# First FFN's end in a two-layer transformer on one NeuronCore: normalised tiles scaled by VectorE and transposed plainly, instead of multiplied by a scaled identity

## The chip, the cores and the metric

The kernel runs on one core of one Trainium2 chip. The metric is device time in microseconds (us) for one execution; less is better. The engines of the core have short names in the profile: PE is TensorE (matmuls; PEld is its weight load), DVE is VectorE, ACT is ScalarE, POOL is GpSimd and SP is SyncE, which here only issues DMAs. Each engine works through its own queue in order, and waits on semaphores where a result of another engine is needed.

## The reference

Two layers over 768 tokens (256 context, 512 latent) of width 1024. Each layer has a mixer and a SwiGLU feed-forward block (FFN), each between two RMS norms:

```python
def _rms(x, gain, eps=1e-6):
    y = xf * lax.rsqrt(jnp.mean(xf * xf, axis=-1, keepdims=True) + eps)
    return y * gain
def _modulate(h, shift, scale):
    return h * (1 + scale) + shift
...
x_lat = x_lat + m_lat[5] * _rms(_swiglu(h_lat, w_gate, w_up, w_down), norm_post_ffn[l])
...
h_lat = _modulate(_rms(x_lat, norm_pre_mix[l]), m_lat[0], m_lat[1])   # next layer
o_ctx, o_lat = _odd_mixer(h_ctx, h_lat, ...)                          # starts with h @ w_in
```

The change is at the seam of the two layers: the end of the first FFN (last assignment), and the norm, modulation and transposition that make `h`, the input of the second layer's mixer.

## The kernel before, in words

Tokens are worked in six tiles of 128, in the order 4, 5 (context), 0, 1, 2, 3 (latent). Products are made in a split form: every float32 operand is a high part and the rest ("H" and "L", `fp32r`), and each product is three matmuls (`mm3`: H by H, H by L, L by H).

The **down product** of the first FFN (`down`) is seven passes of a Strassen scheme. Its result gathers in one tile `y`, [128, 6, 1024], a row of 1024 per token tile, in SBUF. The sixth pass finishes `y` for tiles 4, 5 and 0; the seventh and last finishes it for 1, 2 and 3 (L1798, `y<-y,x`). For each finished tile, `end` queues a small chain of work, `post_pre`:

- a DMA on SP loads the residual, `xr<-x` (L1512; four buffers for six tiles),
- `post_norm`: ACT sums the squares of `y` (L676), DVE multiplies by the gate row (`pn<-y,gv`, L746), DVE scales the sum (`ms`, L666), POOL takes the power -1/2 (`rs`, L668), DVE makes `xr = pn*rs + xr` (L755); for latent tiles SP stores it (L1515),
- `pre_norm`: ACT sums the squares of `xr` (L676), DVE and POOL make a second `rs`, and then DVE multiplies the 128x128 identity by `rs`, a row each: `dg` (L689). When two tiles of a pair (4 and 5, 0 and 1, 2 and 3) are ready, their transposition is queued.

`pair_turn` transposes a pair in four steps `q`. In a step PE makes four 128x128 products of a block of `xr` (the stationary operand) and `dg` (the moving one) into one PSUM tile `hT`: that is the transposed block, each token scaled by its `rs`. ACT applies the modulation (two L727, `hf<-hT`) and casts the high part (L734), DVE makes the low part (L735). Only then can the next layer read these 256 columns of the two tiles. `hT` has two PSUM buffers.

The steps are strewn among other matmuls of PE, and this order is written out by hand. The four steps of the pair 4, 5 stand among the last matmuls of the down product's seventh pass (`x`). Then comes `values`, the first product of the second layer's mixer (`nat`): for each of two column halves `c` and each token tile, 24 matmuls over four weight units `i` (each a DMA `raw<-in_odd_w_in`, an ACT cast `wH` L769 and a DVE subtraction `wL` L770). The steps of pair 0, 1 stand in the second token tile of `c = 0`, one after each weight unit; the steps of pair 2, 3 in the fourth. Behind them, DVE sums a modulation vector (`macc`, L595 and L597) from weights that SP loads (L579), and PE turns it near the end of `values` (`mod_acc`).

PE's order and that of DVE, ACT and POOL in this part are those of the program text (they are pinned there); DMAs of SP are placed by the tile framework, by when their buffer comes free.

The normalisation ahead of the FFNs (`forms` in the code) already works with a whole scaled tile: DVE writes `xn = xr * rs` (L695), and PE transposes blocks of it with the plain identity (L358).

Of the kernel before, what the change touches and what calls it, by code (L numbers as in the profile page):

```python
# [8 lines left out]
F32 = mybir.dt.float32  # L9
# [4 lines left out]
ALU = mybir.AluOpType  # L14
# [3 lines left out]
P = 128  # L18
D = 1024
# [297 lines left out]
class Net:  # L317
# [358 lines left out]
        self.nc.scalar.activation(junk, src, AF.Square, accum_out=ss)  # L676
        return ss

    def pre_norm(self, pool, t, xt, A, B, h):

        nc = self.nc
        r = 0 if t < LT else 1
        forms = isinstance(h, Forms)
        xn = pool.tile([P, D], F32, tag="xn", bufs=2, name=f"xn{t}") if forms else None
        rs = self.rstd(self.sumsq(xt, xn), D)
        yield
        if not forms:
            dg = pool.tile([P, P], F32, tag="dg", bufs=4, name=f"dg{t}")
            self.mark = nc.vector.tensor_scalar(dg, self.ident, rs, None, op0=ALU.mult)  # L689
            self.pair.append((xt, dg))  # L690
            if len(self.pair) == 2:
                self.turns.append(self.pair_turn(pool, t - 1, self.pair, A, B, h))
                self.pair = []
            return
        self.mark = nc.vector.tensor_scalar(xn, xt, rs, None, op0=ALU.mult)  # L695

        def turn():
            for hf in range(2):
                pt = self.tr_tile(f"hT{t}{hf}")
                f = h.at(hf, t)  # L700
                for kk in range(4):
                    k = hf * 4 + kk
                    self.tr(pt[:, kk * P : (kk + 1) * P], xn[:, k * P : (k + 1) * P], self.ident)
                for kk in range(4):
                    k = hf * 4 + kk
                    src = pt[:, kk * P : (kk + 1) * P]
                    nc.scalar.activation(f[:, kk, :], src, AF.Identity, bias=B[:, r, k : k + 1], scale=A[:, r, k : k + 1])
                h.put(hf, t)

        self.turns.append(turn)  # L710

    def pair_turn(self, pool, t, pair, A, B, h):

        nc = self.nc
        r = 0 if t < LT else 1
        tok = slice(t * P, t * P + 2 * P)

        for q in range(4):
            pt = self.tr_tile(f"hT{t}{q}").rearrange("p (k i) -> p k i", k=2)
            f = pool.tile([P, 2, 2 * P], F32, tag="hf", bufs=2, name=f"hf{t}{q}")  # L720
            for kk in range(2):
                k = 2 * q + kk
                for a, (xt, dg) in enumerate(pair):
                    self.mm(pt[:, kk, a * P : (a + 1) * P], xt[:, k * P : (k + 1) * P], dg, start=True, stop=True)
            for kk in range(2):
                k = 2 * q + kk
                nc.scalar.activation(f[:, kk, :], pt[:, kk, :], AF.Identity, bias=B[:, r, k : k + 1], scale=A[:, r, k : k + 1])  # L727
            self.latest = self.put(h, slice(2 * q, 2 * q + 2), tok, f)
            if q < 3:
                yield  # L730
# [777 lines left out]
    def post_pre(self, pp, y, t, gvs, xsrc, xdst, nxt, cuts):  # L1508

        nc = self.nc  # L1510
        xt = pp.tile([P, D], F32, tag="xt", bufs=4 if nxt and isinstance(nxt[2], Split) else 2, name=f"xr{t}")
        nc.sync.dma_start(out=xt, in_=xsrc(t))  # L1512

        def store(c):
            nc.sync.dma_start(out=xdst(t)[:, c], in_=xt[:, c])  # L1515

        yield from self.post_norm(y, xt, gvs[0 if t < LT else 1], cuts, xdst and store)
        if nxt is not None:
            A, B, h = nxt
            yield from self.pre_norm(pp, t, xt, A, B, h)  # L1520

    def turn(self, left=0):

# [676 lines left out]
```

## Time and profile before

| | us |
|---|---|
| median of 3 runs | 1691.47 (1688.34 to 1691.84) |
| the profiled execution | 1689.01 |
| its span, first to last instruction | 1686.9 |
| granted TensorE clock, mean | 0.998 |
| PE busy | 1646.0 |
| DVE busy | 1309.3 |
| ACT busy | 920.0 |
| down product's last pass, to values' start | 885.7 to 914.1 |
| first and last matmul with `dg` | 905.2 and 945.0 |
| end of the last `dg` | 933.3 |

A row of a timeline has the start in the span, the length, the engine, the line, the operation, output and inputs by the program's names, the shape, how many equal ones it merges, and in brackets for how long the engine stood idle before it and what ended that. A matmul's length is longer than the distance to the next one, because they are pipelined: starts are what to compare. A `q` behind an engine's name is its queue issuing something.

### The profile page before, as it was taken

Reading aid. Unit: us, or ns where it says so; the run is one execution under the profiler, and the core shown is the slowest. Engines: PE = TensorE matmul, PEld = TensorE weight load, DVE = VectorE, ACT = ScalarE, POOL = GpSimd, SP = SyncE. Lnnn points to the kernel's source line nnn. Section 1 sums busy time; section 2 is a strip of 40 time slices with the busy share of each in tenths; the row PEclk is TensorE's granted clock in tenths of the full one; section 3 lists DMA queues with packets and bytes.
Section 4 is the critical chain, followed back from the end, with each engine's and each line's share of the span. In section 5 each row is a group of like instructions: output and inputs, shape, how many; then the busy total and the mean of one; then the engine's idle time right before and its main releaser. Section 6 shows DMA issues by size and latency. Waiting matters only on the chain.

```text
span 1686.9 us, 32540 instructions
## 1 busy us (share of the span) xinstructions
PE 1646.0 (98%) x13407; PEld 1481.6 (88%) x13407; DVE 1309.3 (78%) x2105; ACT 920.0 (55%) x1560; POOL 124.4 (7%) x129
## 2 busy tenths in 40 slices
PE   7999998999999999999999999999999999999997
PEld 5889987888999999998887888888888899999875
DVE  4889768875898988878667548788774599987987
ACT  4745567836543443445447436566664565555654
POOL 1004210011000000003102000000000100000221
PEclk9999999999999999999999999999999999999999
DMA  9651002164243444348625542121124333333793
GB/s 329 192 155 41 2 27 101 51 211 152 85 140 102 148 149 140 113 149 175 131 91 197 177 125 61 51 64 39 52 65 149 125 113 114 112 101 101 190 198 137
DMA packets 184736, 204.79 MB, mean 121 GB/s; under 512 B 7142, under 2 KB 141836, under 8 KB 184588
## 3 DMA queue, kind: packets, MB, share of 16 engines
q1 hardware_dynamic: 173632, 181.82, 34.4%
q0 software_dynamic: 9024, 17.30, 5.9%
q10 hardware_dynamic: 1932, 3.59, 0.6%
q8 instruction: 105, 1.72, 0.4%
q14 instruction: 43, 0.35, 0.1%
HBM read 193.23 MB, written 9.46 MB: 120 GB/s over the span
## 4 chain that ended last, share of the span: by engine, by line
PE 83%; DVE 8%; ACT 4%; DMA 3%; issue 2%; POOL 1%; DVEq 0%; SPq 0%; POOLq 0%; ACTq 0%
PE nat L355 12%; PE a L355 11%; PE ff L355 8%; PE E L355 8%; PE x L355 7%; PE oproj L355 6%; PE b L355 4%; PE D L355 4%; PE o L355 4%; PE fq L355 3%; PE gqk L355 2%; PE pearly L355 2%; PE S L355 2%; PE poh L355 1%; PE attO L355 1%
## 5 line engine op out<-in xcount | busy, mean ns | idle before, releaser
L355 PE MATMUL nat<-wH,x 128*128 128x256 f32 (+2 forms) x968 | 225.4, 321 | 3.0 <-ACT x L734 2.6
L355 PEld LDWEIGHTS nat<-wH,x 128*128 128x128 f32 x968 | 162.2, 190 | 19.2 <-ACT x L734 3.7
L824 ACT CAST wH<-raw 128x1024 fp32r<-128x1024 f32 x120 | 125.4, 1054 | 94.7 <-DVE raw L849 31.7
L825 DVE TENSOR_TENSOR wL<-raw,wH 128x1024 fp32r<-128x1024 f32 x120 | 145.6, 1220 | 20.4 <-ACT wH L824 19.9
L355 PE MATMUL nat<-wL,x 128*128 128x256 f32 (+2 forms) x484 | 153.4, 317 | 0.3 <-DVE wL L770 0.3
L770 DVE TENSOR_TENSOR wL<-raw,wH 128x1024 fp32r<-128x1024 f32 (+1 forms) x83 | 98.7, 1197 | 46.7 <-ACT wH L769 45.8
L355 PE MATMUL ff<-x,wH 128*128 128x512 f32 (+1 forms) x512 | 127.7, 340 | 0.0
L668 POOL TENSOR_TENSOR rs<-ms,neghalf 128x1 f32<-128x1 f32 (+2 forms) x62 | 66.5, 1077 | 783.3 <-DVE ms L666 783.2
L769 ACT CAST wH<-raw 128x1024 fp32r<-128x1024 f32 (+1 forms) x83 | 85.0, 1036 | 69.8 <-PE ff L355 19.8
L355 PE MATMUL oproj<-wH,x 128*128 128x512 f32 x320 | 102.2, 395 | 0.6 <-ACT x L1290 0.6
L597 DVE SCALAR_TENSOR_TENSOR macc<-mraw,scT,macc 128x1024 f32<-128x1024 f32 x70 | 88.2, 1279 | 13.8 <-DMA mraw<-in_mod_w_dram 13.6
L355 PEld LDWEIGHTS nat<-wL,x 128*128 128x128 f32 x484 | 92.1, 190 | 6.0 <-DVE wL L770 0.7
L355 PEld LDWEIGHTS ff<-x,wH 128*128 128x128 f32 x512 | 87.3, 190 | 10.0
L355 PE MATMUL x<-wH,two 128*128 128x512 f32 x280 | 90.5, 392 | 0.9 <-DVE y L1798 0.7
L976 ACT COPY qkh<-arr 128x512 f32<-128x512 f32 x112 | 70.2, 644 | 36.2 <-DVE arr L981 32.1
L1723 POOL DMA_DIRECT2D t<-in_ffn_w_down_dram x36 | 41.8, 1225 | 648.0 <-DVE wL L1757 610.7
L355 PE MATMUL ff<-x,wL 128*128 128x256 f32 (+1 forms) x256 | 86.2, 337 | 0.0
L849 DVE TENSOR_TENSOR raw<-raw 128x512 f32<-128x512 f32 x120 | 82.7, 689 | 2.8
L981 DVE TENSOR_TENSOR arr<-arr,f 128x512 f32<-128x512 f32 x112 | 74.1, 686 | 1.9 <-ACT qkh L976 0.3
L355 PE MATMUL E<-x,wH 128*128 128x384 f32 (+1 forms) x320 | 70.9, 311 | 0.0
L355 PEld LDWEIGHTS oproj<-wH,x 128*128 128x128 f32 x320 | 59.5, 188 | 12.8 <-ACT x L1290 1.2
L355 PE MATMUL a<-x,dH 128*128 128x384 f32 (+1 forms) x320 | 70.4, 309 | 0.2 <-ACT early L897 0.2
(420 smaller groups left out, 4544.6 us busy)
## 6 DMA issues: line engine op xcount, KB each, us to landing
mraw<-in_mod_w_dram SPq DMA_DIRECT2D x80, 512.0 KB, 4.4
raw<-in_ffn_w_gate_dram SPq DMA_DIRECT2D x44, 512.0 KB, 4.9
raw<-in_ffn_w_up_dram SPq DMA_DIRECT2D x44, 512.0 KB, 4.3
raw<-in_odd_w_in_dram SPq DMA_DIRECT2D x40, 512.0 KB, 3.7
t<-in_ffn_w_down_dram POOLq DMA_DIRECT2D x30, 512.0 KB, 7.8
raw<-in_ffn_w_down_dram SPq DMA_DIRECT2D x28, 512.0 KB, 7.5
mraw<-in_mod_w_dram SPq DMA_DIRECT2D x32, 256.0 KB, 6.0
raw<-in_even_w_in_dram SPq DMA_DIRECT2D x16, 512.0 KB, 3.9
```

The lines of the kernel that those rows point to most:

```text
L355: return self.pin(self.nc.tensor.matmul(*a, **k))
L597: nc.vector.scalar_tensor_tensor(a, u, w, a, op0=ALU.mult, op1=ALU.add)
L668: nc.gpsimd.tensor_tensor(rs, ms, self.neghalf.to_broadcast([P, w]), op=ALU.pow)
L769: nc.scalar.copy(H[:, :m], raw[:, :m])
L770: nc.vector.tensor_tensor(L[:, :m], raw[:, :m], H[:, :m].bitcast(F32), op=ALU.subtract)
L824: self.nc.scalar.copy(H, f)
L825: self.nc.vector.tensor_tensor(L, f, H.bitcast(F32), op=ALU.subtract)
L849: add = lambda o, x, y: nc.vector.tensor_tensor(o, x, y, op=ALU.add)
L976: nc.scalar.copy(qkv[:, :, :, half, :], dst)
L981: nc.vector.tensor_tensor(dst, dst, tb, op=ALU.mult)
L1723: add = lambda o, src: self.pin(nc.gpsimd.dma_start(out=o, in_=src, accum_op=ALU.add))
```

## The change

DVE now multiplies the whole tile `xr` (128x1024) by `rs`, and writes the result over that tile's row of `y`, which nothing needs any more. PE transposes blocks of it with the unscaled identity, as transposes and not as products. The rest of `pair_turn` is as it was. `dg` and its buffers are gone.

```diff
-    def pre_norm(self, pool, t, xt, A, B, h):
+    def pre_norm(self, pool, t, xt, A, B, h, xn):
...
         forms = isinstance(h, Forms)
-        xn = pool.tile([P, D], F32, tag="xn", bufs=2, name=f"xn{t}") if forms else None
-        rs = self.rstd(self.sumsq(xt, xn), D)
+        if forms:
+            xn = pool.tile([P, D], F32, tag="xn", bufs=2, name=f"xn{t}")
+        rs = self.rstd(self.sumsq(xt, xn if forms else None), D)
         yield
         if not forms:
-            dg = pool.tile([P, P], F32, tag="dg", bufs=4, name=f"dg{t}")
-            self.mark = nc.vector.tensor_scalar(dg, self.ident, rs, None, op0=ALU.mult)
-            self.pair.append((xt, dg))
+            self.mark = nc.vector.tensor_scalar(xn, xt, rs, None, op0=ALU.mult)
+            self.pair.append(xn)
...
-                for a, (xt, dg) in enumerate(pair):
-                    self.mm(pt[:, kk, a * P : (a + 1) * P], xt[:, k * P : (k + 1) * P], dg, start=True, stop=True)
+                for a, xn in enumerate(pair):
+                    self.tr(pt[:, kk, a * P : (a + 1) * P], xn[:, k * P : (k + 1) * P], self.ident)
...
-            yield from self.pre_norm(pp, t, xt, A, B, h)
+            yield from self.pre_norm(pp, t, xt, A, B, h, y)
```

On PE, a step's four products become four transposes at the same place; this is the first step, of tiles 4 and 5 (`xr_9419` and `xr_9451`), among the matmuls of the down product's last pass:

```order
 L355 MATMUL x_8499<-wH,two 128x512
-L355 MATMUL hT_9584<-dg_9495,xr_9419 128x128
-L355 MATMUL hT_9584<-dg_9560,xr_9451 128x128
-L355 MATMUL hT_9584<-dg_9495,xr_9419 128x128
-L355 MATMUL hT_9584<-dg_9560,xr_9451 128x128
+L358 MATMUL hT_9582<-ident,y_8479 128x128 x4
 L355 MATMUL x_8499<-wH,aH 128x512
```

Nothing else on PE has moved.

On DVE, `dg` is replaced where it stood; this is tile 4's, between the down product's operands and the residual sum of tile 5:

```order
 L1757 TENSOR_TENSOR wL<-raw,wH 128x1024
 L1758 TENSOR_TENSOR two<-zy,two 128x768
-L689 TENSOR_SCALAR dg_9495<-ident,rs 128x128
+L689 TENSOR_SCALAR y_8479<-xr_9419,rs 128x1024
 L755 SCALAR_TENSOR_TENSOR xr_9451<-pn,rs,xr_9451 128x1024
 L746 TENSOR_TENSOR pn<-y_8479,gv_9347 128x1024
```

One instruction is eight times as wide; no other has moved on DVE, and none on ACT and POOL.

On SP's queue at the same place, the loads of the fifth and sixth residual tile (`xr<-x`) wait for a free buffer of four. Before, a buffer came free with the last product of its pair on PE; now it does with DVE's scaling:

```order
L768 DMA raw<-in_odd_w_in_dram 128x2x512 x4
L1515 DMA x_96<-xr_9510 128x1024
L768 DMA raw<-in_odd_w_in_dram 128x2x512
L1512 DMA xr_9702<-x_95 128x1024
L1512 DMA xr_9736<-x_95 128x1024
L1515 DMA x_96<-xr_9577 128x1024
```

That was before; this is the same stretch of SP's queue with the change (`xr_9699` and `xr_9732` are the fifth and sixth tile here):

```order
L768 DMA raw<-in_odd_w_in_dram 128x2x512 x2
L1512 DMA xr_9699<-x_95 128x1024
L768 DMA raw<-in_odd_w_in_dram 128x2x512 x2
L1512 DMA xr_9732<-x_95 128x1024
L1515 DMA x_96<-xr_9509 128x1024
L768 DMA raw<-in_odd_w_in_dram 128x2x512 x2
```

The two loads have moved ahead, the one past three weight loads and a store, the other past one of each.

## The prediction

> **What bounds the kernel now.** I read the page first, then the chain of waits, then the busy times by stage around the change, and what PE waits for there.
>
> ```profile
> span 1686.9 us, 32540 instructions
> PE 1646.0 (98%) x13407; PEld 1481.6 (88%) x13407; DVE 1309.3 (78%) x2105; ACT 920.0 (55%) x1560; POOL 124.4 (7%) x129
> PE 83%; DVE 8%; ACT 4%; DMA 3%; issue 2%; POOL 1%; DVEq 0%; SPq 0%; POOLq 0%; ACTq 0%
> ```
>
> PE is the bound over the whole span, and holds 83% of the chain that ended last. So a PE instruction taken away is time gained, except where PE would then wait. The windows (PE, PEld, DVE, ACT and POOL busy, clock, DMA share, GB/s) cover the last pass of the down product and `values`:
>
> ```profile
> 895.00:905.00 10.00, 8.08 (x35) 6.12 (x34) 8.88 (x13) 4.54 (x7) 3.86 (x4) 1.00 0.48 133
> 905.00:919.00 14.00, 13.71 (x77) 11.60 (x75) 9.74 (x15) 12.13 (x22) 1.94 (x2) 1.00 0.48 168
> 919.00:923.00 4.00, 3.05 (x14) 2.38 (x14) 3.26 (x6) 2.52 (x5) 0.94 (x2) 1.00 0.98 339
> 923.00:937.40 14.40, 14.40 (x78) 12.44 (x79) 7.15 (x12) 10.05 (x19) 1.74 (x4) 1.00 0.55 198
> 937.40:945.30 7.90, 7.90 (x52) 7.12 (x52) 1.90 (x3) 4.94 (x9) 0.00 (x0) 1.00 0.01 2
> PE x L355 <- DVE wL L1757: 1.6, 1, 1.6
> PE hT L355 <- DVE dg L689: 0.9, 1, 0.9
> PE nat L355 <- DVE wL L770: 0.3, 1, 0.3
> ```
>
> The change acts in 50 us, and in two kinds of stage. Up to 923 PE waits three times for DVE, and in the second window ACT is busy for 12.13 of 14 us: there the chain through ACT and DVE is as long as PE's own work. From 923 on PE never idles, and from 937.4 DVE and ACT have room.
>
> **The change on PE.** A step of `hT` before, a step of plain transposes of the same shape elsewhere (in the first layer), and the totals:
>
> ```profile
> 905.18 1.05 PE L355 MATMUL hT<-dg,xr 128*128 128x128 f32 x8
> 905.99 0.48 PE L355 MATMUL x<-wH,aH 128*128 128x512 f32 x1
> 379.02 1.03 PE L358 MATMUL hT<-ident,xn 128*128 128x128 f32 x8
> L355 PE MATMUL hT<-dg,xr x96: 270/275/377, 905.2 to 945.0; 128*128 128x128 f32 x96
> L358 PE MATMUL hT<-ident,xn x80: 270/273/330, 379.0 to 1349.9; 128*128 128x128 f32 x80
> ```
>
> A float32 product is two records: 12 steps of four products are 48, and 96 stand there. A transpose is one: ten tiles of eight blocks are 80. Eight records of either kind take the same time (1.05 and 1.03), so a record costs the same. A step takes 0.81 (905.18 to the next matmul at 905.99), or 0.11 a record with the last one overlapped. With four records it is 0.36, so 0.45 less, and 12 steps give 5.4 us less PE work. That is the most the change can give.
>
> **The change on DVE and POOL.** The scaling of 128 columns becomes one of 1024:
>
> ```profile
> L689 DVE TENSOR_SCALAR dg<-ident,rs x6: 280/286/287, 896.4 to 933.0; 128x128 f32<-128x128 f32 x6
> L695 DVE TENSOR_SCALAR xn<-xr,rs x10: 742/753/755, 372.7 to 1347.1; 128x1024 f32<-128x1024 f32 x10
> ```
>
> L695 is the same operation in the same shape: 0.75 for 0.29, or 0.47 more, six times, 2.8 us in all. It also meets POOL, since in four of six cases POOL's next `rs` starts just ahead of the scaling. The rows: POOL alone, under a wide scaling already running, and with a scaling that starts midway.
>
> ```profile
> 909.33 0.55 POOL L668 TENSOR_TENSOR rs<-ms,neghalf 128x1 f32<-128x1 f32 x1 [5.81 <-DVE ms L666]
> 7.25 0.75 DVE L1891 TENSOR_SCALAR xt<-xt,rs 128x1024 f32<-128x1024 f32 x1
> 7.39 1.02 POOL L668 TENSOR_TENSOR rs<-ms,neghalf 128x1 f32<-128x1 f32 x1 [0.73 <-DVE ms L666]
> 301.44 1.28 POOL L668 TENSOR_TENSOR rs<-ms,neghalf 128x4 f32<-128x4 f32 x1 [45.73 <-DVE ms L666]
> 302.08 0.61 DVE L198 TENSOR_SCALAR prob<-prob,ars 128x768 f32<-128x768 f32 x1
> ```
>
> Under a running scaling POOL takes 1.02, and ends 0.41 behind it (8.41 against 8.00). Where the scaling begins during it, POOL ends right behind it (302.72 against 302.69). The `rs` here starts some 0.07 ahead of the scaling (at 896 below: 894.04 + 2.84 - 0.55 = 896.33, `dg` at 896.40), so I take the second case, an end 0.04 behind the scaling. The bounds are no wait at all (0.55) and the first case (0.41 behind). They change the sum below at two places, tiles 4 and 1: no wait gives 0.16 back at each, and 2.9 in place of 2.6; the first case takes 0.37 more at each, and 1.9 is left.
>
> [...]
>
> **Tile 4's scaling, at 896.**
>
> ```profile
> 894.04 2.84 POOL L668 TENSOR_TENSOR rs<-ms,neghalf 128x1 f32<-128x1 f32 x2 [4.67 <-DVE ms L666]
> 896.40 0.29 DVE L689 TENSOR_SCALAR dg<-ident,rs 128x128 f32<-128x128 f32 x1 [0.44 <-POOL rs L668]
> 896.92 1.28 DVE L755 SCALAR_TENSOR_TENSOR xr<-pn,rs,xr 128x1024 f32<-128x1024 f32 x1 [0.23 <-POOL rs L668]
> 900.53 0.50 PE L355 MATMUL x<-wL,aH 128*128 128x512 f32 x1 [1.56 <-DVE wL L1757]
> ```
>
> The scaling now lasts to 897.15, the second `rs` to 897.19, and L755, which starts 0.04 behind it as before, starts at 897.23: 0.32 later. Behind it in DVE's queue, with no idle time between, are `pn`, the `wL` that PE waits for and the next `aL`; PE waits 0.32 longer. (With no wait of POOL it would be 0.16, with the first case 0.69.)
>
> **The pair 4, 5, and two gates.**
>
> ```profile
> 906.27 1.03 ACT L727 ACTIVATE hf<-hT,modcol,aff 128x256 f32<-128x256 f32 x2 [1.10 <-PE hT L355]
> 912.16 1.03 ACT L727 ACTIVATE hf<-hT,modcol,aff 128x256 f32<-128x256 f32 x2 [0.64 <-PE hT L355]
> 917.76 1.22 DVE L770 TENSOR_TENSOR wL<-raw,wH 128x1024 fp32r<-128x1024 f32 x1
> 919.03 0.50 PE L355 MATMUL nat<-wL,x 128*128 128x512 f32 x1 [0.32 <-DVE wL L770]
> 922.64 0.28 DVE L689 TENSOR_SCALAR dg<-ident,rs 128x128 f32<-128x128 f32 x1 [0.67 <-POOL rs L668]
> 922.98 0.94 PE L355 MATMUL hT<-dg,xr 128*128 128x128 f32 x6 [0.92 <-DVE dg L689]
> ```
>
> By 919 PE has gained 4 x 0.45 - 0.32 = 1.5. But the fourth weight unit (917.76) must be there too, and it hangs on ACT, which works without a pause except for PE at 906.27 and 912.16. The first start comes 0.13 earlier (0.32 later, 0.45 shorter), and the second wait (0.64) goes, so ACT is 0.77 ahead. Tile 0's wider scaling, in DVE's queue ahead of that `wL`, takes 0.10 of it and the rest of its 0.47 falls into DVE's own waits for ACT. So the gate at 919 moves by 0.67, and PE waits there for the rest. Next comes tile 1's scaling, 0.67 earlier but 0.47 longer: the `hT` at 922.98 moves by only 0.20. Of 1.8 us on PE 0.2 are left.
>
> **The pair 0, 1, and a new wait.** PE does three transposes at 922.78 and three more steps: 0.20 + 0.33 + 3 x 0.45 = 1.9 ahead. But what the third token tile of `nat` reads last, step 4's low part, still hangs on DVE and ACT:
>
> ```profile
> 929.64 1.06 ACT L676 ACTIVATE junk<-xr 128x1024 bf16<-128x1024 f32 x1 [0.37 <-DVE xr L755]
> 933.97 0.69 DVE L735 TENSOR_TENSOR x<-hf,x 128x512 fp32r<-128x512 f32 x1 [0.69 <-ACT x L734]
> 935.18 0.62 PE L355 MATMUL nat<-wH,x 128*128 128x512 f32 x2
> ```
>
> The matmul at 935.18 is the first to read it (third of the unit i = 3). It is ready at 934.66, 0.52 ahead. The `xr` behind tile 1's scaling starts 0.35 earlier (0.67, less 0.32 as at 896), ACT's sum waits for it, and steps 3 and 4 are behind that in ACT's queue: the low part comes 0.35 earlier. PE can move by 0.52 - 0.05 (signal) + 0.35 = 0.82 and then waits, where it did not before.
>
> **The pair 2, 3.** Tile 3's `dg` starts at 933.0 (L689's row), its steps at 937.4, and ACT is busy for 4.94 of the 7.90 us: nothing new is waited for, and 4 x 0.45 = 1.8 stay.
>
> **What moves with it at no cost.** The loads of `xr` for tiles 2 and 3 go out earlier, and on SP's queue the weight loads behind them now wait for tile 4's and 5's scaling too. They wait for a later instruction of DVE anyway (first row below). Writing over `y` makes no new wait: its readers (`pn`, the sum of squares) are through before `xr`, which the scaling reads. Behind 945 PE works alone to 983, where `mod_acc` reads DVE's last `macc`:
>
> ```profile
> SPq L768 <- DVE wL L1757: 13.9, 3, 6.2
> 947.66 1.41 DVE L595 TENSOR_SCALAR macc<-mraw,scT 128x1024 f32<-128x1024 f32 x2
> 979.45 1.28 DVE L597 SCALAR_TENSOR_TENSOR macc<-mraw,scT,macc 128x1024 f32<-128x1024 f32 x1 [1.70 <-DMA mraw<-in_mod_w_dram]
> 983.32 1.06 PE L355 MATMUL mod_acc<-macc,one 128*32 128x512 f32 x8
> ```
>
> It is 2.6 ahead (980.73), and its chain begins behind the last step's L735, which comes 2.6 earlier as well. I take no loss there.
>
> **Sum:** 0.82 + 1.80 = 2.6 us less. The profiled execution took 1689.01, 2.1 of them outside the span, so 1686.4 for one like it. The median of the runs stands 2.5 above it; from the median it is 1688.9.
>
> **The rivals.**
>
> *PE's gain is kept* (22 in 100). If ACT or DVE get more forward than I count, the gates at 919, 923 and 935 move as well. Without the last, it is 1.9 + 1.8 = 3.7; with all, 5.4: 1687.8 to 1686.1. For it: gates are close (0.32, 0.92 and 0.52). Against it: two of three hang on DVE, which gets more work.
>
> *DVE and POOL become the bound* (13 in 100, the other side). Each wide scaling costs DVE 0.47 more, and holds POOL's next `rs` as at 7.39 for 0.47 more. If DVE had no slack from 896 to 935, five tiles (4, 5, 0, 1, 2) cost 2.35, and the four with an `rs` behind them 1.88; the pair 2, 3 gives back 1.8: 2.4 slower, 1693.9. It decides when DVE's waits for ACT between 905 and 919 are used up. Against it: DVE is idle there for 14 - 9.74 = 4.3 us. [...]
>
> *Transposes cost as much in place as the products* (7 in 100): a step is then bounded by the switch between operand kinds, PE gains nothing, and the delays of 0.32 and 0.47 stay: 0.5 to 0.8 slower, 1692.1. Against it: eight transposes between matmuls at 379 show no such price.
>
> The rest of my chances: 48 for the forecast, 10 for what I don't see.
>
> **Range and chances.** 0.2% is 3.4 us, about what a measurement of this kernel can tell from no change, as the three runs lie 3.5 apart. The forecast lies inside; with that spread I give three tenths of its 48 to faster, 19 of the kept gain's 22 and 2 of the unseen: 36. Slower by over 3.4 needs the DVE bound (6 of 13) or costly transposes (2 of 7) plus the spread, or something unseen (6): 14. Within: 50. The range of 8 in 10 leaves out most of the DVE bound and of the unseen: from 1685.8 (all of 5.4, and a little spread) to 1692.4 (transposes not cheaper).
>
> **What would show it.** 48 records of `hT` with 0.11 from start to start; L689 at 0.75; L755 at 896.9 about 0.3 later; PE's wait at 919 and 922.8 longer (1 to 2 us) instead of shorter; a new wait near 934 for L735; the steps of pair 2, 3 1.8 us shorter in sum, with no wait. I am wrong if PE does not wait at 934, if `rs` behind a scaling takes over 1.0, or if the time behind 945 differs.

## The result, and the profile after

Over 20 runs each, the kernel after takes 1688.41 us in the median (1684.80 to 1690.33) where the kernel before takes 1690.95 (1688.34 to 1692.09), 2.5 us less; the ratio on record is 0.9987, with a 95% interval of 0.9981 to 0.9993, or 1.2 to 3.2 us less. The forecast was 2.6 us less. In a second set of runs the ratio was 0.9988 (0.9980 to 0.9997), and the medians differed by 2.2 us.

The two profiled executions alone would mislead. Their spans, 1686.9 and 1686.5, differ by only 0.4 us:

```profile
span 1686.5 us, 32442 instructions
PE 1643.9 (97%) x13359; PEld 1476.2 (88%) x13359; DVE 1311.9 (78%) x2105; ACT 916.5 (54%) x1560; POOL 125.8 (7%) x129
```

The counts say what changed (48 records less on PE), but the execution after ran 1.04 us late before it came to the change (POOL's `rs` ahead of tile 4's scaling starts at 895.08, before at 894.04), and it lost another 0.85 behind 985, at several small steps in places that the change doesn't touch. So from here on times are counted from that `rs` in each profile, and the *stretch* is the time from it to the start of `mod_acc`, where all of the change lies behind: 983.32 - 894.04 = 89.28 before, 982.08 - 895.08 = 87.00 after, or 2.28 less.

The rows that answer to the prediction's, first the windows and PE's waits from 880 to 1000 (for what it waited, us in total, times, longest), then rows of the timeline, in the last block those of PE and DVE together:

```profile
905.00:919.00 14.00, 13.29 (x67) 10.69 (x65) 11.54 (x16) 12.88 (x22) 2.41 (x3) 1.00 0.55 176
919.00:923.00 4.00, 2.95 (x12) 2.13 (x12) 3.33 (x7) 2.60 (x5) 0.65 (x2) 1.00 0.85 295
923.00:937.40 14.40, 13.40 (x62) 10.02 (x63) 8.77 (x13) 10.01 (x19) 2.65 (x4) 1.00 0.55 185
937.40:945.30 7.90, 7.90 (x45) 6.53 (x44) 2.08 (x3) 6.34 (x12) 0.00 (x0) 1.00 0.00 0
PE x L355 <- DVE wL L1757: 1.9, 1, 1.9
PE hT L358 <- DVE y L689: 1.5, 1, 1.5
PE nat L355 <- DVE wL L770: 1.0, 1, 1.0
```
```profile
898.26 1.28 DVE L755 SCALAR_TENSOR_TENSOR xr<-pn,rs,xr 128x1024 f32<-128x1024 f32 x1
913.36 0.60 PE L358 MATMUL hT<-ident,y 128*128 128x128 f32 x4
913.71 0.48 PE L355 MATMUL nat<-wH,x 128*128 128x512 f32 x1
...
919.33 0.50 PE L355 MATMUL nat<-wL,x 128*128 128x512 f32 x1 [1.04 <-DVE wL L770]
...
922.35 1.37 POOL L668 TENSOR_TENSOR rs<-ms,neghalf 128x1 f32<-128x1 f32 x2 [7.71 <-DVE ms L666]
922.93 0.75 DVE L689 TENSOR_SCALAR y<-xr,rs 128x1024 f32<-128x1024 f32 x1 [0.67 <-POOL rs L668]
923.74 0.55 PE L358 MATMUL hT<-ident,y 128*128 128x128 f32 x3 [1.47 <-DVE y L689]
```
```profile
932.52 0.98 PE L355 MATMUL nat<-wH,x 128*128 128x512 f32 x2
932.98 0.69 DVE L735 TENSOR_TENSOR x<-hf,x 128x512 fp32r<-128x512 f32 x1 [1.41 <-ACT x L734]
933.33 0.40 PE L355 MATMUL nat<-wL,x 128*128 128x512 f32 x1
933.72 0.72 PE L355 MATMUL nat<-wH,x 128*128 128x512 f32 x2
...
934.55 0.69 DVE L735 TENSOR_TENSOR x<-hf,x 128x512 fp32r<-128x512 f32 x1 [0.22 <-ACT x L734]
...
934.98 0.40 PE L355 MATMUL nat<-wL,x 128*128 128x512 f32 x1
935.30 0.73 PE L355 MATMUL nat<-wH,x 128*128 128x512 f32 x2
```

A step takes 0.35 us instead of 0.81 (913.36 to 913.71). The wait for `wL` at 919 has grown from 0.3 to 1.0, the one for the scaling at 922 from 0.9 to 1.5: PE arrives earlier, and what it waits for does not come as much earlier. In the window from 923 PE was busy all of 14.40 us and is now for 13.40, but that is not the new wait: 0.74 of the 1.00 is the end of the gate at 922, which lies in this window now (up to 923.74), and 0.16 a short wait for an `hT` buffer at 927.52. The new wait hardly shows as idle time, since matmuls overlap (a row of one is 0.39 to 0.40 long, at 0.23 from start to start, as from 912.20 to 912.66); the starts show it. From 932.52 to 935.86, eleven matmuls take 3.34 us where the same eleven took 2.50 before (932.45 to 934.95), so 0.84 is lost (a pair `x2` lasts 0.98 or 0.73 where 0.62 is normal). PE's weight loads wait there twice for DVE's low part (L735; 0.8 in all) and once for ACT's cast (L734; 0.5), which they did not before; the starts of 933.72 and 935.30 stand just behind the two low parts (932.98 to 933.67 and 934.55 to 935.24). From 937.40 PE has no idle time, as before.

### The profile page after: what moved, and what is told of

Same layout as the page of the kernel before. It is cut to its first block, busy times and chain, and to the rows that moved or that the text cites. A ratio compares the mean times of both kernels' runs of the same rounds, so it can differ in the third digit from the quotient of the medians.

```text
span 1686.5 us, 32442 instructions
## 1 busy us (share of the span) xinstructions
PE 1643.9 (97%) x13359; PEld 1476.2 (88%) x13359; DVE 1311.9 (78%) x2105; ACT 916.5 (54%) x1560; POOL 125.8 (7%) x129
## 4 chain that ended last, share of the span: by engine, by line
PE 83%; DVE 7%; ACT 4%; DMA 3%; issue 2%; POOL 1%; DVEq 0%; ACTq 0%; POOLq 0%
PE a L355 12%; PE nat L355 11%; PE ff L355 8%; PE E L355 8%; PE x L355 7%; PE oproj L355 5%; PE o L355 4%; PE D L355 4%; PE b L355 4%; PE fq L355 3%; PE gqk L355 2%; PE pearly L355 2%; PE S L355 2%; PE poh L355 1%; PE attO L355 1%
## 5 line engine op out<-in xcount | busy, mean ns | idle before, releaser
L597 DVE SCALAR_TENSOR_TENSOR macc<-mraw,scT,macc 128x1024 f32<-128x1024 f32 x70 | 88.1, 1279 | 14.2 <-DMA mraw<-in_mod_w_dram 14.1
L355 PE MATMUL ff<-x,wL 128*128 128x256 f32 (+1 forms) x256 | 86.2, 337 | 0.0
L355 PE MATMUL a<-T,wH 128*128 128x384 f32 (+1 forms) x320 | 70.6, 309 | 0.1
```

The source lines that it names most:

```text
L355: return self.pin(self.nc.tensor.matmul(*a, **k))
L597: nc.vector.scalar_tensor_tensor(a, u, w, a, op0=ALU.mult, op1=ALU.add)
```

## Experiments

"Fall" says whether PE's granted clock fell to 0.50 behind its wait at 900, which the second profile of the kernel after brought to light (below). It costs some 1.3 us, so a stretch is compared with one of the same kind: 87.00 for a profile without, 88.09 for one with a fall. The profiles of the experiments come from three chips (e6, e8 and e9 from a second one, e10 from a third). Five with a fall and the same work up to there, from two of the chips (after, e3, e6, e8, e9), have the first step of `hT` 12.67 to 12.70 us behind the `rs`.

| kernel | stretch | fall | median of its runs | ratio to before (95%) |
|---|---|---|---|---|
| before, two profiles | 89.28, 89.18 | no, no | 1690.95 | |
| after, two profiles | 87.00, 88.09 | no, yes | 1688.41, 1687.97 | 0.9987 (0.9981 to 0.9993), 0.9988 (0.9980 to 0.9997) |
| e1, VectorE's half | 91.26 | yes | 1691.15 | 1.0007 (0.9998 to 1.0016) |
| e2, last pair only | 89.02 | yes | 1689.18 | 0.9998 (0.9989 to 1.0007) |
| e3, first two pairs only | 89.77 | yes | 1690.83 | 0.9997 (0.9988 to 1.0006) |
| e4, PE's half | 86.28 | no | 1687.95 | 0.9989 (0.9980 to 0.9998) |
| e5, tile 3's sum left out | 85.88 | no | 1686.97 | 0.9983 (0.9974 to 0.9992) |
| e6, tile 1's scaling split | 88.01 | yes | 1688.76 | 0.9991 (0.9983 to 1.0000) |
| e7, each scaling twice | 92.16 | longer | 1692.49 | 1.0014 (1.0005 to 1.0023) |
| e8, tile 1 by products | 87.78 | yes | 1687.87 | 0.9985 (0.9976 to 0.9993) |
| e9, and two casts on DVE | 87.44 | yes | 1687.52 | 0.9984 (0.9975 to 0.9993) |
| e10, and weights first | 85.32 | no | 1685.59 | 0.9973 (0.9964 to 0.9982) |

The whole times have intervals of 1.5 us to either side; they can confirm e7 and e10, but not part the others. Those are judged by the stretch and the rows in it, from one profile each.

### Both kernels again

> The kernel before once more, for a second profile. All theories: the stretch from POOL's rs ahead of tile 4's scaling to the start of mod_acc takes 89.28 us again (983.32 - 894.04), to 0.1 us; the span outside it may differ by 1 us. If the stretch itself differs by more than 0.3 between the two profiles, what is read from single rows here is within the noise.

> The kernel after once more, in the same rounds as the experiments. Theory of the gates (PE's shorter steps are given back where PE waits for work of VectorE and ScalarE, and 2.3 to 2.6 of 5.4 us stay): the stretch from POOL's rs to mod_acc takes 87.00 us again (982.08 - 895.08), and the ratio to the kernel before is near 0.9985. Rival (the 2.5 us are no property of this place): the stretch differs by more than 0.3 us, or the ratio is 1.000.

Before: 89.18, within 0.10 of the first profile. After: 88.09, or 1.09 more than in the first, and this from a single place. Windows of the second profile and of the first (PE, PEld, DVE, ACT, POOL busy, then the granted clock):

```profile
900.00:902.00 2.00, 1.31 (x3) 0.78 (x4) 2.00 (x5) 0.24 (x1) 0.53 (x1) 0.67 0.32 32
902.00:904.00 2.00, 2.00 (x6) 1.58 (x5) 1.56 (x3) 0.00 (x0) 1.75 (x2) 0.50 0.85 261
904.00:906.00 2.00, 2.00 (x10) 1.63 (x9) 1.92 (x3) 1.15 (x2) 0.00 (x0) 0.98 0.95 309
```
```profile
902.00:904.00 2.00, 1.63 (x6) 1.10 (x7) 1.94 (x4) 0.00 (x0) 1.11 (x1) 1.00 0.49 106
904.00:906.00 2.00, 2.00 (x10) 1.68 (x9) 1.62 (x3) 0.17 (x1) 1.17 (x2) 1.00 0.75 207
```

Behind the wait of 1.9 us for `wL` the clock is 0.50 for 3.4 us, matmuls follow each other at 0.43 instead of 0.23, and the first step of `hT` stands 12.70 behind the `rs` instead of 11.43. The 1.27 stays (1.30 at the last step of `hT`). The other 0.21 is a pause of PE at 957 in the first profile, which the second does not have: there a `macc` (L597), waiting for its DMA, stood in DVE's queue ahead of a weight unit's `wL`. So without fall and pause the gain of the stretch is 2.5, with the pause 2.3. The expectation that the stretch repeats within 0.3 failed; its reading, that the 2.5 us are no property of this place, does not follow, because but for these two places the stretch repeats within 0.05.

### One half alone, then the other

e1 keeps the wide scaling, but turns by products as before:

```diff
-                    self.tr(pt[:, kk, a * P : (a + 1) * P], xn[:, k * P : (k + 1) * P], self.ident)
+                    self.mm(pt[:, kk, a * P : (a + 1) * P], xn[:, k * P : (k + 1) * P], self.ident, start=True, stop=True)
```

> The VectorE half alone: whole tiles are scaled, but turned by products with the identity (two records each) as before. Theory of the gates: against the kernel before, tile 4's scaling makes PE 0.32 later, the gate at 919 is 0.35 to 0.42 later, the gate at 922 0.85, there is no new wait at 934, and 0.85 stays to the end: the stretch to mod_acc takes 90.1 us (89.28 + 0.85), some 3.1 above the kernel after, near 1691.8 by the median. Rival 'VectorE is the bound' (it had no slack): 2.4 to 4.2 slower than before. Rival 'VectorE's part costs nothing': 89.3, as before.

e4 keeps the transposes, with a scaling as narrow as before (the other 896 columns are left out):

```diff
-            self.mark = nc.vector.tensor_scalar(xn, xt, rs, None, op0=ALU.mult)
+            self.mark = nc.vector.tensor_scalar(xn[:, :P], xt[:, :P], rs, None, op0=ALU.mult)
```

> The PE half alone: plain transposes, but VectorE scales only the first 128 columns of each tile (0.29 us as before); the scaling of the other 896 columns is left out, so the hidden layer's input is another one. Theory of the gates: the gates at 919 and 922 come 1.1 earlier than in the kernel before, the third token tile of nat (934) 1.5, and the pair 2, 3 adds 1.8: 3.1 to 3.4 less than before at mod_acc, a stretch of 85.9 to 86.2, about 0.9 below the kernel after. So PE's half would lose 2 of 5.4 us even with VectorE's work unchanged. Rival 'PE's gain is kept but for VectorE's longer work': 5.4 less than before, a stretch of 83.9.

The `rs` and the start of `mod_acc` in e1, then in e4, there with two of PE's waits:

```profile
893.03 3.15 POOL L668 TENSOR_TENSOR rs<-ms,neghalf 128x1 f32<-128x1 f32 x2 [4.67 <-DVE ms L666]
984.30 1.06 PE L355 MATMUL mod_acc<-macc,one 128*32 128x512 f32 x8
```
```profile
894.69 2.85 POOL L668 TENSOR_TENSOR rs<-ms,neghalf 128x1 f32<-128x1 f32 x2 [4.67 <-DVE ms L666]
980.96 1.06 PE L355 MATMUL mod_acc<-macc,one 128*32 128x512 f32 x8
PE hT L358 <- DVE y L689: 1.0, 1, 1.0
PE nat L355 <- DVE wL L770: 0.9, 1, 0.9
```

e1 (first fence) is 3.17 above the kernel after with a fall, where 3.1 was expected. Less the 2.3 to 2.5 that the kernel after gains, it is 0.7 to 0.9 slower than before (0.85 expected; the medians say 0.9, with an interval that holds no change too). VectorE's half alone costs under 1 us, not 2.4: it is not the bound. e4 (second fence) is 3.0 below the kernel before; it has the pause at 957 too (0.3 us). So even with VectorE's work unchanged, 5.4 us less PE work bring 3.0 to 3.3: PE waits 0.9 at 919 and 1.0 at 922, where it waited 0.3 and 0.9. The gates lose the larger part, VectorE's longer work the smaller one.

### One stage alone, then the others

In e2 only tiles 2 and 3, in e3 only the other four are scaled whole and transposed; the rest goes by `dg` and products as before. The edit of e3 in `pre_norm` (e2 has the other tiles in the list; `pair_turn`, not shown, makes a transpose where there is no `dg`, and a product where there is one):

```diff
-            self.mark = nc.vector.tensor_scalar(xn, xt, rs, None, op0=ALU.mult)
-            self.pair.append(xn)
+            if t in (4, 5, 0, 1):
+                self.mark = nc.vector.tensor_scalar(xn, xt, rs, None, op0=ALU.mult)
+                self.pair.append((xn, None))
+            else:
+                dg = pool.tile([P, P], F32, tag="dg", bufs=4, name=f"dg{t}")
+                self.mark = nc.vector.tensor_scalar(dg, self.ident, rs, None, op0=ALU.mult)
+                self.pair.append((xt, dg))
```

> Only tiles 2 and 3 are scaled whole and turned by transposes; tiles 4, 5, 0 and 1 go by products with the scaled identity as before. Theory of the gates: nothing waits there, so all of 4 x 0.45 = 1.8 us stays: the stretch to mod_acc takes 87.5 (89.28 - 1.8), or 87.7 if the 0.2 that the kernel after lost behind this place is lost here too. Rival 'the gain of the last pair is taken back by the chain of macc behind 945': 89.3, and the wait of mod_acc for DVE is longer.

> The complement: tiles 4, 5, 0 and 1 go by transposes, 2 and 3 by products. Theory of the gates: 3.6 us less PE work, of which 0.8 to 0.9 stays, the rest being waited at 919, 922 and 934 as in the kernel after: a stretch of 88.4. The gains of the two complements add up to the whole change's (2.3). Rival 'PE's gain is kept': 3.6, a stretch of 85.7.

Both profiles have a fall, and the kernel before has none to compare with. But the fall is over ahead of the first step of `hT`, so the time from there to `mod_acc` compares: 78.14 before (905.18 to 983.32), 76.39 in e2 (905.87 to 982.26), 77.09 in e3 (906.65 to 983.74). e2 is 1.75 shorter, on 1.8 expected. e3 is 1.05 shorter, and its first step is 0.31 later by the wait at 900: 0.74, on 0.8 to 0.9 expected and 3.6 by the rival. Their sum, 2.5, is the whole change's gain. Of the 1.8 us that each pair saves on PE, the last pair keeps all, the other two together keep 0.74 of 3.6.

### What holds PE near 934

e5 leaves ACT's sum of squares of tile 3 out:

```diff
-        rs = self.rstd(self.sumsq(xt, xn if forms else None), D)
+        rs = self.rstd(self.one if not forms and t == 3 else self.sumsq(xt, xn if forms else None), D)
```

> The kernel after, with ACT's sum of squares of tile 3 left out (a constant takes its place, so tile 3's scaling is another number); it stands at 930.23 in ACT's queue, takes 1.15 us, and steps 3 and 4 of the pair 0, 1 stand behind it. Theory of the gates (PE waits near 934 for the low parts of steps 3 and 4, which hang on ACT's queue): the low parts come 1.4 earlier, PE's gaps between 933 and 936 go, and the stretch is 0.9 to 1.1 shorter than the kernel after's 87.0: 85.9 to 86.1. Rival (what holds PE there is not ACT's queue): within 0.2 of 87.0.

DVE's low parts of steps 3 and 4 in e5, and the PE rows that answer to 932.52 and 935.30 of the kernel after:

```profile
929.77 0.69 DVE L735 TENSOR_TENSOR x<-hf,x 128x512 fp32r<-128x512 f32 x1 [0.59 <-ACT x L734]
...
931.34 0.69 DVE L735 TENSOR_TENSOR x<-hf,x 128x512 fp32r<-128x512 f32 x1 [0.22 <-ACT x L734]
930.83 0.62 PE L355 MATMUL nat<-wH,x 128*128 128x512 f32 x2
...
932.87 0.62 PE L355 MATMUL nat<-wH,x 128*128 128x512 f32 x2
```

The low parts come 36.37 and 37.95 behind the `rs`, 1.5 earlier than in the kernel after (37.90 and 39.47); PE's matmuls now follow at the normal distance from 928.77 to 934.91, and the stretch is 85.88: 1.12 shorter, or 0.9 without the pause at 957, which e5 does not have; the new wait cost 0.84. PE waited there for ACT's queue.

e6 opens the gate at 922 earlier and leaves the chain behind it alone; e8 shortens that chain as well, and gives PE more work:

```diff
-            self.mark = nc.vector.tensor_scalar(xn, xt, rs, None, op0=ALU.mult)
+            for c in [slice(0, 256), slice(256, D)] if t == 1 else [slice(0, D)]:
+                self.mark = nc.vector.tensor_scalar(xn[:, c], xt[:, c], rs, None, op0=ALU.mult)
```

> The kernel after, with tile 1's scaling written in two pieces, the first 256 columns and then the other 768, so that the first transposes of the pair 0, 1 need only the first piece. Theory of the gates (a gate that opens earlier only moves the wait to the next one, here the low parts at 934): the hT at 922 starts 0.4 earlier than in the kernel after, PE waits that much more near 934, since xr behind the scaling starts no earlier (0.1 to 0.2 later, for one more instruction), and the stretch is 0 to 0.2 longer than 87.0. Rival (the gate at 922 is where the time goes): 0.4 shorter, 86.6.

```diff
-            if t in (4, 5, 0, 1):
+            if t != 1:
```

(the second one is e3's edit with another list of tiles)

> The kernel after, but tile 1 alone goes by the scaled identity and products: a step of the pair 0, 1 has two transposes and two products (6 records, 0.58 us). Theory of the gates: the hT at 922 starts 0.47 earlier than in the kernel after, and xr behind the scaling 0.3 earlier, since POOL's rs is not held; so the gate at 934 opens 0.3 earlier, and the stretch is 0.3 shorter although PE has 4 x 0.22 = 0.9 us more work: 86.7. Rival (PE's own work counts, not the chain through xr): 0.9 longer, 87.9.

```profile
PE hT L358 <- DVE y L690: 1.1, 1, 1.1
PE nat L355 <- DVE wL L771: 1.0, 1, 1.0
PE hT L358 <- ACT hf L728: 0.6, 1, 0.6
922.38 0.90 DVE L690 TENSOR_SCALAR y<-xr,rs 128x256 f32<-128x256 f32 x2 [0.67 <-POOL rs L668]
923.20 1.27 DVE L756 SCALAR_TENSOR_TENSOR xr<-pn,rs,xr 128x1024 f32<-128x1024 f32 x1
```
```profile
922.30 0.29 DVE L694 TENSOR_SCALAR dg<-ident,rs 128x128 f32<-128x128 f32 x1 [0.67 <-POOL rs L668]
922.82 1.28 DVE L764 SCALAR_TENSOR_TENSOR xr<-pn,rs,xr 128x1024 f32<-128x1024 f32 x1 [0.23 <-POOL rs L668]
```

In e6 (first fence) `hT` behind the gate starts 0.40 earlier than in the kernel after (29.53 for 29.93, all with a fall), and the wait comes back at once, for an `hT` buffer that ACT still reads (0.6 instead of 0.2): stretch 88.01 for 88.09, no gain. In e8 (second fence) `xr` starts 0.52 behind `dg`, not 0.83 behind the scaling (922.93 and 923.76 in the kernel after): 29.62 behind the `rs`, not 29.95. The stretch is 87.78, 0.31 shorter, although PE has 8 records more. So what counts here is when `xr` starts on DVE, not what PE has to do.

### Twice the scaling

```diff
+            nc.vector.tensor_scalar(xn, xt, rs, None, op0=ALU.mult)
             self.mark = nc.vector.tensor_scalar(xn, xt, rs, None, op0=ALU.mult)
```

> The kernel after, with each of the six scalings written twice, one behind the other: 0.75 us more on DVE each. Theory of the gates, with POOL's rs held as long as scalings run: the rs that starts just ahead takes 1.6 instead of 0.86 and ends 0.04 behind the second scaling; tile 4's adds 0.75 to PE's wait at 900, tile 0's another 0.75 to the gate at 919, tile 1's another 0.75 at 922, the other three nothing: the stretch is 2.2 longer than the kernel after's, 89.2, about the kernel before. Rival 'VectorE is the bound throughout': 6 x 0.75 = 4.5 longer, 91.5. Rival 'VectorE is off the path': within 0.3 of 87.0. If POOL slips in between the two scalings, rs takes 0.86 to 1.0 and ends before the second one ends.

PE's waits, two windows, and the second `rs` beside tile 1's two scalings:

```profile
PE x L355 <- DVE wL L1758: 2.5, 1, 2.5
PE hT L358 <- DVE y L690: 2.3, 1, 2.3
902.00:908.00 6.00, 5.93 (x14) 4.46 (x14) 5.44 (x9) 1.15 (x2) 2.28 (x2) 0.50 0.74 202
930.00:935.00 5.00, 5.00 (x26) 4.21 (x24) 4.02 (x7) 4.27 (x8) 1.37 (x2) 0.81 0.17 70
925.36 1.37 POOL L668 TENSOR_TENSOR rs<-ms,neghalf 128x1 f32<-128x1 f32 x2 [8.50 <-DVE ms L666]
925.95 0.75 DVE L689 TENSOR_SCALAR y<-xr,rs 128x1024 f32<-128x1024 f32 x1 [0.67 <-POOL rs L668]
926.74 0.75 DVE L690 TENSOR_SCALAR y<-xr,rs 128x1024 f32<-128x1024 f32 x1
```

The stretch is 92.16, 4.07 above the kernel after with a fall, and not 2.2. Read alone, this would be nearly the 4.5 of the rival. Place by place it is not: the gate theory's three steps are there (0.63 at the `xr` behind tile 4's scaling, 0.79 more at the gate at 919, 0.80 more at 922, in all 2.2), and nearly all of the rest is clock. The wait at 900 is now 2.5 and the clock stays at 0.50 up to 908 (1.3 us more than in the kernel after with a fall), and behind the wait of 2.3 at 922 it falls a second time. That place holds the remaining 0.5, and what the other three scalings cost cannot be told from it: `xr` of tile 3 stands 5.43 behind that of tile 2, and 5.17 in the kernel after, so up to 0.3 may be theirs. POOL's second `rs` ends at 926.73 (925.36 + 1.37), 0.03 behind the *first* scaling, just ahead of the second one: it slips in between, and is not held for as long as scalings follow each other.

### A version that goes around the gates

e9 is e8 with the casts of two steps (L734) on DVE; this is the part that it adds:

```diff
-            self.latest = self.put(h, slice(2 * q, 2 * q + 2), tok, f)
+            self.latest = self.put(h, slice(2 * q, 2 * q + 2), tok, f, t >= LT and q < 2)
...
-        cast = self.nc.scalar.copy(H, f)
+        cast = (self.nc.vector.tensor_copy if dve else self.nc.scalar.copy)(H, f)
```

> As the one with tile 1 by products, and the casts of the high parts of steps 1 and 2 of the pair 4, 5 done by DVE, which idles there (gaps of 0.6 and 1.4 us at 908 and 911), instead of ACT, which has none. Theory of the gates: ACT and DVE come 0.5 us further by 919, the gates at 919, 922 and 934 all open 0.5 earlier, and the stretch is 0.8 to 0.9 shorter than the kernel after's: 86.1 to 86.2, some 3.1 below the kernel before, 1687.8. Rival (DVE is as full as ACT there): as with tile 1 alone, 86.7, or longer by DVE's two casts of 0.62.

The stretch is 87.44 with a fall: 0.65 below the kernel after with one, where 0.8 to 0.9 was expected; 0.34 of it is by the casts, of which 0.5 was expected. The gain shows at 919 (PE waits 0.8 for `wL`, not 1.0).

e10 is e9 with the last weight unit of the down product written ahead of one step of the small chain, in the seventh pass:

```diff
                 if p == 6:
+                    if not l and (g, i) == (tail - 1, nh - 1):
+                        ahead(3)
                     self.tick()
```

> As the one with tile 1 by products and two casts on DVE, and the last weight unit of the down product (wL and aL, with their casts on ACT) placed ahead of tile 0's pn and sum of squares, which nothing needs so early. Theory of the clock (PE's wait of 1.94 to 2.25 us at 900 lets the granted clock fall to 0.50 for some 3 us in most executions, 1.1 to 1.3 us each time): wL is there 1.22 earlier, PE waits 1.0 there instead of 2.25, the clock stays at 1.00 between 900 and 906, and the stretch is 1.1 to 1.3 shorter than that kernel's 87.44: 86.2 to 86.4; the gates behind take the rest of the 1.22. By the median about 0.8 less than it, some 1686.7, ratio 0.9980. Rival (the fall of the clock comes at that place whatever the wait): the clock falls again, and the stretch is 87.2 to 87.4.

```profile
899.98 1.22 DVE L1766 TENSOR_TENSOR wL<-raw,wH 128x1024 fp32r<-128x1024 f32 x1
901.11 0.95 DVE L1767 TENSOR_TENSOR aL<-qb,aH 128x768 fp32r<-128x768 f32 x1
901.98 1.22 DVE L755 TENSOR_TENSOR pn<-y,gv 128x1024 f32<-128x1024 f32 x1
PE x L355 <- DVE wL L1766: 0.7, 1, 0.7
902.00:904.00 2.00, 1.88 (x8) 1.59 (x9) 2.00 (x5) 0.18 (x1) 0.59 (x1) 1.00 0.84 223
904.00:906.00 2.00, 2.00 (x11) 1.60 (x11) 1.56 (x3) 0.00 (x0) 1.69 (x2) 1.00 0.40 68
```

`wL` now stands ahead of `pn`, PE waits 0.7 us instead of 1.9, and the clock stays at 1.00. The stretch is 85.32, 2.1 below e9 and 1.7 below the kernel after without a fall, and the runs take 1685.59 us in the median, 0.9973 (0.9964 to 0.9982) of the kernel before. That is more than was expected (86.2 to 86.4): the gates did not take the rest of the 1.22. Tile 1's `xr` on DVE, just ahead of the gate at 919, starts 20.05 behind the `rs`, 22.19 in e9: 1.3 of it is the clock, 0.9 got through. That the clock stays up is read from one profile; whether it does in other executions was not shown. e10 is faster than the kernel before by 4.2 us in its own set of runs, the kernel after by 2.5 and 2.2 in its two. So it beats the kernel after by about 2 us, though the two were not run in one set and their intervals touch.

## Why the prediction was right

The forecast was 1688.9 us within 1685.8 to 1692.4, most likely no change of over 0.2%. The runs say 1688.41, 0.13% less by the ratio. The interval of 1.2 to 3.2 us is wide, so that the median came within 0.1 us of the forecast 2.6 is in part luck; the steps are the better test. The steps, each as how much earlier than in the kernel before, counted from the `rs`, in the profile without a fall:

| step | predicted | measured |
|---|---|---|
| `xr` (L755) behind tile 4's scaling | -0.32 | -0.30 |
| gate at 919, fourth weight unit | 0.67 | 0.74 |
| gate at 922, tile 1's scaling | 0.20 | 0.28 |
| third token tile of `nat`, behind the new wait | 0.82 | 0.92 |
| behind the last step of the pair 2, 3 | 2.62 | 2.53 |
| `mod_acc` | 2.62 | 2.28 |

- **PE's records.** 48 for 96, a step 0.35 for 0.81: as predicted. That transposes cost as much as products in place is refuted; a step bounded by a switch between operand kinds shows in no run.
- **DVE and POOL.** L689 takes 0.75, and the `rs` that starts ahead of it 0.86, ending 0.04 behind it: the value taken between the bounds of 0.55 and 1.02 was right at all places where it counted; the first case (0.41 behind), which would have left 1.9, did not come. Where an `rs` starts under another wide operation and the scaling follows, it takes longer (912.96 to 914.64, 1.69, before 1.39); nothing waits for that one.
- **The gates.** All three held where they were put and to 0.1 us. e4 shows them without VectorE's part, e3 and e2 that the loss lies ahead of 937 and the gain behind it, e1 that VectorE's part alone costs 0.7 to 0.9. The kept gain (rival one) and VectorE as the bound (rival two) are refuted.
- **The new wait.** It was put at step 4's low part. The rows show it for step 3's as well (933.72), and a sum of squares in ACT's queue that it hangs on is that of tile 3, which waits for tile 3's `xr`; the prediction had quoted that sum as the one behind tile 2's `xr`. The two `xr` stand 5.17 apart in both kernels, so the wrong one moves by as much as the right one, and the time came out near all the same (0.46 earlier measured for step 4's low part, 0.35 predicted). e5 shows the dependence.
- **Behind 945.** "No loss there" was off by 0.2 in one of two profiles: PE waits at 957 for a weight unit that stands on DVE behind a `macc` whose data is late.
- **What the prediction did not see** is the clock. It took 1.00 in the windows of one profile for a property of the place, and priced PE's longer wait at 900 at its 0.32. In the second profile of the kernel after, that place costs 1.3 more. Neither profile of the kernel before has it, though e2, with the same wait of 1.6, does. How often either kernel's executions have the fall was not measured, so its share in the medians' 2.5 and 2.2 is not known; the sum of 2.6 leaves it out.

## What to carry to other kernels

Before a faster instruction on the busiest engine is booked as a gain, follow each place where that engine next waits, and ask what moves the releaser: here 5.4 us less PE work became 2.5, because three waits in a row hang on a chain through VectorE and ScalarE that PE's speed moves little. Opening one of these gates alone moves the wait to the next one (e6); shortening the chain is what counts (e5, e8), and the cheapest way was an operand that PE needs, put ahead of one that nobody needs yet (e10); 1.3 of its 2.1 us are the clock that it keeps up. Compare two profiles between anchors close to the change, more than once: the spans differed by 0.4 us where the place had gained 2.3.

## What the runs showed of the hardware

- The granted clock fell to 0.50 behind PE's wait at 900 in eight of the 14 profiles, and the kernel after did it in one execution and not in the other. By the length of that wait in the view of waits: 0.7 us, no fall (e10); 1.6 us, one in four (e2, not the kernel before twice nor e4); 1.9 us, six in eight (not the first profile of the kernel after nor e5); 2.5 us, one of one (e7). By the windows, e7's fall lasted 6.8 us, the seven others 3.4 us each, and these cost 1.2 to 1.5 us each. The waits of 1.0 to 1.5 at 919 and 922 had no fall in any of them.
- The length of the wait alone does not decide: waits of 1.6 and of 1.9 us stand here with a fall and without one. What decides beside it was not shown. e10 has another fall far from the change (clock 0.83 in the window from 100 to 110, PE busy for 8.15 of its 10 us); the two profiles of the kernel before, the two of the kernel after, and e9 have 1.00 in that window, with PE busy for 8.25 to 8.38.
- A float32 transpose and one of the two records of a float32 product take the same 0.11 us from start to start, and the granted clock of the kernel after stayed at 1.00 through the steps of transposes, in both profiles.
- A narrow POOL operation that starts 0.07 ahead of a wide scaling of DVE ends 0.03 to 0.04 behind it (0.86 for 0.55); it is not held by a second scaling of the same tile right behind the first (e7), nor by one split in 256 and 768 columns, of which the second piece follows without a gap (e6: both `rs` together 1.06, as before the change). Why the split one lets it through was not tried.
